# A hybrid encoder layer: background work paced by estimated VectorE time, eight gate tiles moved to seven-product blocks, and an earlier reload of m

## The chip, the cores and the metric

One core of a Trainium2 chip runs the whole kernel. TensorE (PE in the profile, PEld for its weight loads) multiplies, VectorE (DVE) and ScalarE (ACT) do element-wise work, GpSimd (POOL) and SyncE (SP) mostly issue transfers. The metric is the device time of one execution in microseconds; the median of the runs counts, lower is better.

## What is computed

One layer with two mixers, for 512 positions of width 2048, in float32, followed by a final RMSNorm:

```python
h = rmsnorm(x, norm_g)
v, bg, cg, za, u, zb, ga, gb = split(h @ w_in)        # 2048 x (4*2048, 2*1024, 2*2048)
ya = ((bg * causal_conv3(cg * v)) * silu(za)) @ w_out_a
yb = gelu(s5_scan(u))                                  # 64 groups, 16 channels, 64 complex states
yb = yb * sigmoid(yb @ w_glu + b_glu)
yb = (yb * silu(zb)) @ w_out_b
m  = sigmoid(ga) * ya + sigmoid(gb) * yb
out = rmsnorm(x + m @ w_o, final_g)
```

## The kernel before

**Arithmetic.** Every operand of a matmul is split into a rounded part `hi` and a remainder `lo`; a product is hi*hi + hi*lo + lo*hi. Activations lie transposed (channels on partitions, the 512 positions along a row), in `pair` tiles with both parts. A weight slot holds 128 x 1024 numbers: one block of 128 output channels by half of the 2048 inputs.

**Weights.** `WStream` walks a fixed list of weight slots. SP loads a raw slot (`w_raw`), ACT rounds it to `w_hi` (L545), DVE subtracts to get `w_lo` (L562). There are four buffers each of `w_hi` and `w_lo`, and `get` prepares two slots ahead of the one in use.

**A plain tile** of 128 outputs takes two `gemm` calls (one for each half of the inputs), each 8 x 3 matmuls of 128x512 (L700 to L702). `gate` (L824 to L828) computes one such tile of g_a or g_b, applies tanh on ACT (L827) and stores it to DRAM from POOL's queue (L828). g_b comes back as `tmp<-gb`, g_a as `ga_r`.

**A block of seven** (`seven`, `product`) computes two tiles at once by seven products instead of eight (a Strassen-Winograd scheme over two output tiles, two input halves and two halves of the positions). A `product` is 8 matmuls of 128x512 (L931) and 8 of 128x256 (L936). DVE forms four sums and differences of weights for each block (`add7`, L492 to L501); ACT copies partial results out of PSUM (L946, L949, L951, L962), DVE adds them into `half` tiles and into the result. The sums of activations (`th7`, `ty7`) are made once by `combine`.

**The stages in order**: u projection and RMSNorm (0 to 98 us); stage 1, plain tiles: 12 tiles of g_a, 16 of g_b, 8 of z_b; the GLU product; W_out_b, 16 tiles of one gemm, then two more tiles of g_a; the four projections cg, v, za, bg in 32 blocks of seven, each group of four followed by convolution, silu and product; the last two tiles of g_a; W_out_a, four plain tiles and six blocks of seven (`wa`), with `mix` forming m and storing it to DRAM; the output projection with W_o, which needs m back from DRAM as `pair` tiles (`reload_m`, tile `m_r`), and the final norm.

**The background.** Work that is not matmul of the main line is written as generators in a list `bg`. `step(n)` is called after each gemm or product and runs generators up to their next `yield`, strictly in list order. In stage 1 the background is the S5 branch: parameters (`ssm_params`), four blocks of 16 groups (`ssm_blocks`), and `gelu`. For each block `front` fetches u and parameters through POOL's queue and prepares small matrices on DVE (`F`, L48 with names `ssm_f`, `ssm_ft`), `pe1` and `pe2` issue the branch's own matmuls, `post` spreads results on ACT, and `scan` builds a rotation table (`ssm_rr`, `ssm_ri`), turns the states, runs the recurrence (L416) and turns them back. `pe2` writes its output to the tile `uy` through POOL's queue. Before the change `step` counted yields:

```python
    def step(n=1.0):
        owed[0] += n
        while owed[0] >= 1.0:
            owed[0] -= 1.0
            while bg:
                try:
                    next(bg[0])
                    break
                except StopIteration:
                    bg.pop(0)
```

The order of the instructions on each engine is fixed when the kernel is built: it follows the order of the program, except that an instruction for which nothing is missing may be put ahead of an earlier one that is expected to wait. An engine then executes its list in order. Two pools of buffers bind too: `c.r4` with 37 slots (raw weights, pairs, all S5 tiles), and `r4b` with 6 slots, from which `wide` tiles come (results of blocks, `half`, `m_r`, `ga_r`, `tb_r`).

Of the kernel before, what the change touches and what calls it, by code (L numbers as in the profile page):

```python
# [16 lines left out]
P = 128  # L17
# [7 lines left out]
T = 4  # L25
# [3 lines left out]
MAGIC = 12582912.0  # L29
RATE = 2.75  # L30
PRATE = 1.0
WARM = 9
NR4 = 37
NA = 12
NAB = 14
NP7 = 4
HL = L // 2

# [3 lines left out]


def _ew(nc):
    v = nc.vector

    def tt(o, a, b, op):
        return v.tensor_tensor(out=o, in0=a, in1=b, op=op)  # L48
# [189 lines left out]
class Block:  # L238
# [13 lines left out]
    def front(self):  # L252
# [22 lines left out]
        shp = [P, QB, NC]  # L275
        ft = self.new([P, QB, 5, NC], "ft")
        for ri in range(2):
            f = self.new([P, QB, 5, NC], "f")
            for tau in range(5):
                pr = c.pw[:, tau, 0, q0:q0 + QB].unsqueeze(2).to_broadcast(shp)  # L280
                pi = c.pw[:, tau, 1, q0:q0 + QB].unsqueeze(2).to_broadcast(shp)
# [97 lines left out]
    def scan(self):  # L379
# [33 lines left out]
        for q in range(QB):  # L413
            g = c.mag[:, q0 + q:q0 + q + 1].to_broadcast([P, NCH])
            for h in (hr, hi):
                nc.vector.tensor_tensor_scan(out=h[:, q, :], data0=g, data1=h[:, q, :],  # L416
                                             initial=0.0, op0=MUL, op1=ADD)
            if q % 2:
                yield
# [159 lines left out]
def hybrid_kernel(ctx: ExitStack, tc: tile.TileContext, xT, x, cvec, fg, wu, wu7, wabc,  # L579
# [63 lines left out]
    for j in range(NAB, KD):  # L643
        for h in range(2):
            W.add(wga[j, h])
# [37 lines left out]

    def step(n=1.0):
        owed[0] += n
        while owed[0] >= 1.0:
            owed[0] -= 1.0
            while bg:
                try:
                    next(bg[0])  # L690
                    break
                except StopIteration:
                    bg.pop(0)

# [104 lines left out]
    def gelu(m):  # L799
        y = uy[:, m].rearrange("p s k -> p k s")  # L800
        t, u = tmp(), tmp()
        t3, u3 = (v.rearrange("p (k s) -> p k s", s=T) for v in (t, u))
        act.activation(t3, y, AF.Square)
        ts(t, t, 0.044715, MUL, 1.0, ADD)
        tt(t3, t3, y, MUL)
        yield
        act.activation(u, t, AF.Tanh, scale=0.7978845608028654)
        stt(t3, u3, 1.0, y, ADD, MUL)
        g = pair()
        split(g, t)  # L810
        yg.append(g)
        yield
# [92 lines left out]
    for j in range(KD):  # L905
        ps = psum()
        gemm(ps, yb, steps=1.2)
        th = gq[j]
# [3 lines left out]
    for j in range(NA, NAB):  # L912
        gate(ga_d[j // 2][:, j % 2], 2.0)
    while bg:
# [6 lines left out]

    def product(ps, acts, first, last, steps=1.0):

# [15 lines left out]

    def seven(name, acts, steps=1.0):  # L940

# [43 lines left out]
    def out_a(cc, b, j):  # L985
        tt(b, b, cc, MUL)
        nc.gpsimd.dma_start(yag_d[j // 2], b)
        yield

    hb = blocks(hp, th7)  # L990
    for j in range(0, KD, 2):
# [58 lines left out]

    def reload_m(i):
        t = wide("m_r")
        nc.gpsimd.dma_start(t, m_d[i])
# [195 lines left out]
```

## Time and profile before

| | before |
|---|---|
| median of three runs | 1692.85 us (1689.97 to 1694.98) |
| profiled execution | 1694.92 us, its span 1693.1 us |
| mean granted TensorE clock | 0.995 |
| PE, DVE, ACT, POOL busy | 99%, 76%, 43%, 8% of the span |
| HBM read and written | 203.1 and 24.8 MB, 135 GB/s |

The profiled execution is one run. A busy PE is a PE with a matmul in its pipeline; the mean duration of one matmul (390 ns) is longer than the distance between two starts (227 ns), since they overlap. Lines of the page name the source line, the engine, the tile written and the tiles read. An idle time is put down to what ended it last.

### The profile page before, as it was taken

What the parts mean: (1) busy time and instruction counts of PE and PEld (TensorE: products, weight loads), DVE (VectorE), ACT (ScalarE), POOL (GpSimd) and SP (SyncE); (2) the same over time, 40 slices, a digit from 0 to 9 for tenths busy, and PEclk for the clock granted to TensorE, in tenths of its full rate; (3) what the DMA queues carried; (4) which work ended last, traced back from release to release, by engine and by line L of the source; (5) the groups of instructions that cost most, each with busy time, mean ns of one, the idle gap of its engine ahead of it and who ended that gap; (6) DMA issues with size and microseconds to landing.
All of it is one profiled execution on the core that took longest, in us unless ns stands there. A gap on an engine that the chain in (4) does not pass through costs nothing.

```text
span 1693.1 us, 22360 instructions
## 1 busy us (share of the span) xinstructions
PE 1675.1 (99%) x8612; PEld 1434.0 (85%) x8612; DVE 1286.4 (76%) x1889; ACT 722.4 (43%) x941; POOL 138.9 (8%) x240
## 2 busy tenths in 40 slices
PE   9999999999999999999999999999999999999997
PEld 7888888888888888888888888888888888878887
DVE  7895483948769777698989899998989699974333
ACT  6433423334316422454545554445545444453321
POOL 0003203040100021000000000000000220020000
PEclk9999999999999999999999999999999999999999
DMA  8324345353531454233333433333343855576212
GB/s 303 112 89 133 102 147 113 136 145 103 171 112 54 153 172 157 90 118 116 100 112 102 136 128 108 112 99 115 121 132 130 300 196 179 185 266 256 75 38 100
DMA packets 68331, 233.53 MB, mean 138 GB/s; under 512 B 9152, under 2 KB 9280, under 8 KB 68224
## 3 DMA queue, kind: packets, MB, share of 16 engines
q1 hardware_dynamic: 49392, 170.94, 30.2%
q0 software_dynamic: 18112, 60.06, 11.2%
q8 instruction: 67, 1.10, 0.3%
q10 hardware_dynamic: 720, 1.10, 0.2%
q14 instruction: 40, 0.33, 0.1%
HBM read 203.10 MB, written 24.77 MB: 135 GB/s over the span
## 4 chain that ended last, share of the span: by engine, by line
PE 92%; DVE 4%; DMA 2%; issue 1%; ACT 0%; DVEq 0%; POOL 0%; SPq 0%; ACTq 0%; POOLq 0%
PE ps L931 25%; PE ps L936 13%; PE ps L702 12%; PE ps L701 12%; PE ps L700 12%; PE ps L1103 3%; PE ps L1104 3%; PE ps L1102 3%; PE ps L778 1%; PE ps L779 1%; PE ps L777 1%; DVE w_lo L562 1%; DMA w_raw<-in_wga_dram 1%; PE ps L339 1%; PE ps L434 1%
## 5 line engine op out<-in xcount | busy, mean ns | idle before, releaser
L545 ACT CAST w_hi<-w_raw 128x1024 fp32r<-128x1024 f32 (+2 forms) x347 | 361.7, 1043 | 592.9 <-PE ps L701 246.2
L562 DVE TENSOR_TENSOR w_lo<-w_raw,w_hi 128x1024 fp32r<-128x1024 f32 (+2 forms) x347 | 418.5, 1210 | 242.6 <-ACT w_hi L545 241.9
L700 PE MATMUL ps<-pair,w_hi 128*128 128x512 f32 x912 | 355.8, 390 | 0.0
L702 PE MATMUL ps<-pair,w_lo 128*128 128x512 f32 x912 | 354.4, 389 | 0.7 <-DVE w_lo L562 0.7
L701 PE MATMUL ps<-pair,w_hi 128*128 128x512 f32 x912 | 354.7, 389 | 0.0
L931 PE MATMUL ps<-h_comb,w_hi 128*128 128x512 f32 x1216 | 305.3, 393 | 4.7 <-ACT half L951 4.2
L931 PEld LDWEIGHTS ps<-h_comb,w_hi 128*128 128x128 f32 x1216 | 218.9, 189 | 44.5 <-ACT half L951 4.6
L931 PE MATMUL ps<-pair,w_hi 128*128 128x512 f32 x912 | 230.1, 394 | 0.0
L702 PEld LDWEIGHTS ps<-pair,w_lo 128*128 128x128 f32 x912 | 171.2, 188 | 36.4 <-DVE w_lo L562 1.1
L700 PEld LDWEIGHTS ps<-pair,w_hi 128*128 128x128 f32 x912 | 171.3, 188 | 35.1
L701 PEld LDWEIGHTS ps<-pair,w_hi 128*128 128x128 f32 x912 | 171.3, 188 | 35.1
L931 PEld LDWEIGHTS ps<-pair,w_hi 128*128 128x128 f32 x912 | 165.3, 190 | 29.9
L936 PEld LDWEIGHTS ps<-h_comb,w_lo 128*128 128x128 f32 x1216 | 165.9, 190 | 11.9
L936 PE MATMUL ps<-h_comb,w_lo 128*128 128x256 f32 x1216 | 169.6, 282 | 0.0
L545 ACT CAST w_hi<-w_sum 128x1024 fp32r<-128x1024 f32 x76 | 79.9, 1051 | 139.4 <-DVE w_sum L501 61.5
L936 PEld LDWEIGHTS ps<-pair,w_lo 128*128 128x128 f32 x912 | 125.2, 191 | 9.0
L936 PE MATMUL ps<-pair,w_lo 128*128 128x256 f32 x912 | 127.8, 283 | 0.0
L562 DVE TENSOR_TENSOR w_lo<-w_sum,w_hi 128x1024 fp32r<-128x1024 f32 x76 | 92.6, 1218 | 7.2 <-ACT w_hi L545 7.2
L48 DVE TENSOR_TENSOR half<-ps,half 128x512 f32<-128x512 f32 x114 | 78.0, 684 | 7.2 <-PE ps L936 7.2
L1102 PE MATMUL ps<-w_hi,pair 128*128 128x512 f32 (+1 forms) x212 | 81.6, 385 | 0.0
L1103 PE MATMUL ps<-w_lo,pair 128*128 128x512 f32 (+1 forms) x212 | 81.6, 385 | 0.0
L1104 PE MATMUL ps<-w_hi,pair 128*128 128x512 f32 (+1 forms) x212 | 81.6, 385 | 0.0
(197 smaller groups left out, 1784.5 us busy)
## 6 DMA issues: line engine op xcount, KB each, us to landing
w_raw<-in_wabc_dram SPq DMA_DIRECT2D x128, 512.0 KB, 4.2
w_raw<-in_wga_dram SPq DMA_DIRECT2D x64, 512.0 KB, 4.3
w_raw<-in_wgb_dram SPq DMA_DIRECT2D x48, 512.0 KB, 4.2
w_raw<-in_wo_dram SPq DMA_DIRECT2D x32, 512.0 KB, 7.3
w_raw<-in_wgz_dram SPq DMA_DIRECT2D x24, 512.0 KB, 3.6
w_raw<-in_wu_dram SPq DMA_DIRECT2D x15, 448.0 KB, 7.5
xt<-in_xT_dram SPq DMA_DIRECT2D x16, 256.0 KB, 6.5
ga<-tmp POOLq DMA_DIRECT2D x16, 256.0 KB, 2.4
```

Source lines behind the costliest of these rows:

```text
L48: return v.tensor_tensor(out=o, in0=a, in1=b, op=op)
L339: nc.tensor.matmul(ps[:, i * NCH:(i + 1) * NCH], self.sl[ri][:, q].rearrange("p g s -> p (g s)"), self.u4[:, q, :], start=True, stop=True)
L545: nc.scalar.copy(hi[:, a:b], raw[:, a:b])
L562: nc.vector.tensor_tensor(out=lo[:, a:b], in0=raw[:, a:b], in1=hi.bitcast(F32)[:, a:b], op=SUB)
L700: nc.tensor.matmul(ps, hi[:, k], a[:, 0], start=first and k == 0, stop=False)
L701: nc.tensor.matmul(ps, hi[:, k], a[:, 1], start=False, stop=False)
L702: nc.tensor.matmul(ps, lo[:, k], a[:, 0], start=False, stop=last and k == 7)
L931: nc.tensor.matmul(ps if flat else both, hi[:, k], a, start=first and k == 0, stop=False, skip_group_check=True)
L936: nc.tensor.matmul(ps[:, HL:], lo[:, k], a[:, :HL] if flat else a[:, 0], start=False, stop=last and k == 7, skip_group_check=True)
L1102: nc.tensor.matmul(ps, a[:, 0, cs], hi[:, k2, c0:c1], start=first and k2 == 0, stop=False)
L1103: nc.tensor.matmul(ps, a[:, 0, cs], lo[:, k2, c0:c1], start=False, stop=False)
L1104: nc.tensor.matmul(ps, a[:, 1, cs], hi[:, k2, c0:c1], start=False, stop=last and k2 == 1)
```

## The change

1. **Pacing.** The helpers `tt`, `ts`, `stt` and the scan add an estimate of their VectorE time to `SPENT` (0.1 us and 0.00104 us an element of the row). `step(n)` now runs background until the estimated time of what it ran reaches n, counting at least 0.6 us for each yield. All rates are given anew in that unit.
2. **Gate tiles.** Eight tiles of g_a (6 to 13) are no longer plain: four blocks of seven are inserted among the projections, after the second to the fifth group, with `gate2` for tanh and store. Stage 1 keeps four tiles of g_a, tiles 4 and 5 follow W_out_b, 14 and 15 stay.
3. **Reload of m.** `reload_m(a, b)` issues the loads two blocks ahead of the casts. During the last `wa` block it handles tiles 0 and 1; tiles 2 to 6 come after that block, and so does the last `fetch_m`. The other `fetch_m` calls come one block earlier.
4. **Smaller edits.** `F` is computed with 640 elements a row at once instead of five times 128; `gelu` first copies its operand from the strided `uy` to a contiguous tile on ACT.

```diff
-RATE = 2.75
-PRATE = 1.0
+RATE = 4.75
+PRATE = 2.0
-NA = 12
-NAB = 14
+NA = 4
+NAB = 6
+NB7 = 14
+LEAST = 0.6
+R7, RM7 = 1.2, 1.6
+SPENT = [0.0]
+def spend(ap, n=1):
+    size = 1
+    for d in ap.shape[1:]:
+        size *= d
+    SPENT[0] += n * (0.1 + 0.00104 * size)
...
+        p5 = [c.pw[:, :, i, q0:q0 + QB].rearrange("p t q -> p q t").unsqueeze(3).to_broadcast(sh5) ...]
+        c5 = [v.unsqueeze(2).to_broadcast(sh5) for v in (cr, ci)]
         for ri in range(2):
-            f = self.new([P, QB, 5, NC], "f")
-            for tau in range(5):
-                ...
-                tt(ft[:, :, tau, :], ci, pi if ri == 0 else pr, MUL)
-                tt(f[:, :, tau, :], cr, pr if ri == 0 else pi, MUL)
-                if tau == 2:
-                    yield
+            f = self.new(sh5, "f")
+            tt(ft, c5[1], p5[1 - ri], MUL)
+            tt(f, c5[0], p5[ri], MUL)
+            yield
...
     for j in range(0, KD, 2):                       # order of the weights
         for i in range(4):
             W.add7(wabc[j, i, 0], wabc[j + 1, i, 0], wabc[j + 1, i, 1], wabc[j, i, 1])
+        i = NAB + j - 2
+        if NAB <= i < NB7:
+            W.add7(wga[i, 0], wga[i + 1, 0], wga[i + 1, 1], wga[i, 1])
...
     def step(n=1.0):
         owed[0] += n
-        while owed[0] >= 1.0:
-            ...
+        while owed[0] > 0.0 and bg:
+            t = SPENT[0]
+            try:
+                next(bg[0])
+                owed[0] -= max(SPENT[0] - t, LEAST)
+            except StopIteration:
+                bg.pop(0)
+        owed[0] = min(owed[0], n)
...
     def gelu(m):
-        y = uy[:, m].rearrange("p s k -> p k s")
+        y, t, u = tmp(), tmp(), tmp()
+        act.copy(y.rearrange("p (k s) -> p k s", s=T), uy[:, m].rearrange("p s k -> p k s"))
...
-        gemm(ps, yb, steps=1.2)                     # W_out_b
+        gemm(ps, yb, steps=2.4)
-        gate(ga_d[j // 2][:, j % 2], 2.0)           # tiles NA to NAB
+        gate(ga_d[j // 2][:, j % 2], 3.0)
...
+    def gate2(o, j):
+        t = wide("tz")
+        act.activation(t, o, AF.Tanh, scale=0.5)
+        nc.gpsimd.dma_start(ga_d[j // 2], t)
+        yield
...
         b = seven("bg", hb)
         bg.append(out_a(cc, b, j))
+        i = NAB + j - 2
+        if NAB <= i < NB7:
+            bg.append(gate2(seven("ga", hb), i))
...
-        gemm(ps, yap[:8], last=False, steps=3.2)    # and the second half alike
+        gemm(ps, yap[:8], last=False, steps=3.6)
...
-    def reload_m(i):
-        t = wide("m_r")
-        nc.gpsimd.dma_start(t, m_d[i])
-        yield
-        for n in range(2):
-            p = pair()
-            split(p, t[:, n])
-            mp.append(p)
-            yield
+    def reload_m(a, b):
+        q = []
+        for i in range(a, b + 2):
+            if i < b:
+                q.append(wide("m_r"))
+                nc.gpsimd.dma_start(q[-1], m_d[i])
+                yield
+            if i >= a + 2:
+                t = q[i - a - 2]
+                for n in range(2):
+                    ...
...
+    fetch_m()
     for j in range(NP7, KD, 2):
-        fetch_m()
-        if j == KD - 2:
-            for i in range(4):
-                bg.append(reload_m(i))
-        o = seven("wa", yb7, 2.7 if j == KD - 2 else 1.0)
+        end = j == KD - 2
+        if end:
+            bg.append(reload_m(0, 2))
+        o = seven("wa", yb7, RM7 if end else R7)
+        if end:
+            bg.append(reload_m(2, 7))
+            fetch_m()
+            while bg:
+                step()
+        elif j < KD - 4:
+            fetch_m()
         bg.append(mix(o, *mq[j // 2], j))
-    for i in range(4, 7):
-        bg.append(reload_m(i))
```

More of the change, by code (lines that the diff above doesn't have):

```diff
@@ L47, in tt @@
     def tt(o, a, b, op):
+        spend(o)
         return v.tensor_tensor(out=o, in0=a, in1=b, op=op)
     def ts(o, a, s1, op0, s2=None, op1=None):
+        spend(o)
         if op1 is None:
@@ L55, in stt @@
     def stt(o, a, s, b, op0, op1):
+        spend(o)
         return v.scalar_tensor_tensor(out=o, in0=a, scalar=s, in1=b, op0=op0, op1=op1)
@@ L276, in front @@
         ft = self.new([P, QB, 5, NC], "ft")
+        sh5 = [P, QB, 5, NC]
+        p5 = [c.pw[:, :, i, q0:q0 + QB].rearrange("p t q -> p q t").unsqueeze(3).to_broadcast(sh5)
+              for i in range(2)]
+        c5 = [v.unsqueeze(2).to_broadcast(sh5) for v in (cr, ci)]
         for ri in range(2):
-            f = self.new([P, QB, 5, NC], "f")
-            for tau in range(5):
-                pr = c.pw[:, tau, 0, q0:q0 + QB].unsqueeze(2).to_broadcast(shp)
-                pi = c.pw[:, tau, 1, q0:q0 + QB].unsqueeze(2).to_broadcast(shp)
-                tt(ft[:, :, tau, :], ci, pi if ri == 0 else pr, MUL)
-                tt(f[:, :, tau, :], cr, pr if ri == 0 else pi, MUL)
-                if tau == 2:
-                    yield
+            f = self.new(sh5, "f")
+            tt(ft, c5[1], p5[1 - ri], MUL)
+            tt(f, c5[0], p5[ri], MUL)
+            yield
             if ri == 0:
@@ L415, in scan @@
             for h in (hr, hi):
+                spend(h[:, q, :], 2)
                 nc.vector.tensor_tensor_scan(out=h[:, q, :], data0=g, data1=h[:, q, :],
@@ L642, in hybrid_kernel @@
             W.add7(wabc[j, i, 0], wabc[j + 1, i, 0], wabc[j + 1, i, 1], wabc[j, i, 1])
-    for j in range(NAB, KD):
+        i = NAB + j - 2
+        if NAB <= i < NB7:
+            W.add7(wga[i, 0], wga[i + 1, 0], wga[i + 1, 1], wga[i, 1])
+    for j in range(NB7, KD):
         for h in range(2):
@@ L685, in step @@
         owed[0] += n
-        while owed[0] >= 1.0:
[L687 to L693, printed above, removed]
+        while owed[0] > 0.0 and bg:
[6 more added lines that the diff above has]
+        owed[0] = min(owed[0], n)
     def gemm(ps, acts, first=True, last=True, steps=0.0):
@@ L799, in gelu @@
     def gelu(m):
-        y = uy[:, m].rearrange("p s k -> p k s")
-        t, u = tmp(), tmp()
-        t3, u3 = (v.rearrange("p (k s) -> p k s", s=T) for v in (t, u))
-        act.activation(t3, y, AF.Square)
+        y, t, u = tmp(), tmp(), tmp()
+        act.copy(y.rearrange("p (k s) -> p k s", s=T), uy[:, m].rearrange("p s k -> p k s"))
+        act.activation(t, y, AF.Square)
         ts(t, t, 0.044715, MUL, 1.0, ADD)
-        tt(t3, t3, y, MUL)
+        tt(t, t, y, MUL)
         yield
         act.activation(u, t, AF.Tanh, scale=0.7978845608028654)
-        stt(t3, u3, 1.0, y, ADD, MUL)
+        stt(t, u, 1.0, y, ADD, MUL)
         g = pair()
@@ L920, in blocks, with product @@
         return y + [[sums[k][i] for k in range(8)] for i in range(4)]
-    def product(ps, acts, first, last, steps=1.0):
+    def product(ps, acts, first, last, steps=R7):
         hi, lo = W.get()
@@ L938, in product, with seven @@
         step(steps)
-    def seven(name, acts, steps=1.0):
+    def seven(name, acts, steps=R7):
         Y11, Y21, Y22, T1, T2, T3, T4 = acts
@@ L1018, in hybrid_kernel @@
         step()
-    for j in range(NAB, KD):
-        gate(ga_d[j // 2][:, j % 2], 4.0)
+    for j in range(NB7, KD):
+        gate(ga_d[j // 2][:, j % 2], 3.2)
     while bg:
@@ L1040, in hybrid_kernel @@
         ps = psum()
-        gemm(ps, yap[:8], last=False, steps=3.2)
-        gemm(ps, yap[8:], first=False, steps=3.2)
+        gemm(ps, yap[:8], last=False, steps=3.6)
+        gemm(ps, yap[8:], first=False, steps=3.6)
         g, t = (v[:, j % 2] for v in mq[j // 2])
@@ L1049, in hybrid_kernel @@
     mp = []
-    def reload_m(i):
-        t = wide("m_r")
-        nc.gpsimd.dma_start(t, m_d[i])
-        yield
-        for n in range(2):
-            p = pair()
-            split(p, t[:, n])
-            mp.append(p)
-            yield
+    def reload_m(a, b):
[8 more added lines that the diff above has]
+                for n in range(2):
+                    p = pair()
+                    split(p, t[:, n])
+                    mp.append(p)
+                    yield
     def mix(o, g, t, j):
```

## The prediction

> **What bounds the kernel now.** I read the totals first, then the chain that ended last, the waits of PE, and the busy time by stage.
>
> ```profile
> span 1693.1 us, 22360 instructions
> ...
> PE 1675.1 (99%) x8612; PEld 1434.0 (85%) x8612; DVE 1286.4 (76%) x1889; ACT 722.4 (43%) x941; POOL 138.9 (8%) x240
> ...
> PE 92%; DVE 4%; DMA 2%; issue 1%; ACT 0%; DVEq 0%; POOL 0%; SPq 0%; ACTq 0%; POOLq 0%
> ```
> ```profile
> PE ps L931 <- ACT half L951: 4.2, 1, 4.2
> PE ps L777 <- ACT pair L760: 2.5, 1, 2.5
> ...
> PE ps L702 <- DVE w_lo L562: 0.7, 1, 0.7
> PE ps L931 <- DVE half L48: 0.6, 1, 0.6
> ```
> ```profile
> 98.00:541.00 443.00, 442.31 (x2178) 374.51 (x2177) 306.62 (x692) 164.36 (x228) 79.22 (x125) 1.00 0.40 120
> ...
> 590.00:672.00 82.00, 82.00 (x363) 67.91 (x362) 58.41 (x93) 24.16 (x30) 16.73 (x31) 1.00 0.51 169
> ...
> 694.00:1319.00 625.00, 625.00 (x3583) 550.05 (x3582) 558.79 (x570) 314.42 (x377) 5.34 (x10) 1.00 0.36 118
> ```
> PE is the bound nearly everywhere: it waits about 9 us in all, half of that in one place (ACT's copy at L951, near 1492 us). So the time falls only by matmuls taken away or by that one wait, and rises only where another engine makes PE wait anew. In the third fence each row is a stage: width, then busy PE, PEld, DVE, ACT, POOL. Stage 1 (98 to 541: gates, zb, the S5 background) has DVE 69% busy, the four-projection stage (694 to 1319) 89%.
>
> **The change, part by part.** Price of PE work first. ACT's gate tanh (L827) follows each pair of plain weight tiles; the products of a seven-product block follow each other in the chain.
>
> ```profile
> 282.33 0.60 ACT L827 ACTIVATE tmp<-ps 128x512 f32<-128x512 f32 x1 [4.61 <-PE ps L702]
> 293.21 0.60 ACT L827 ACTIVATE tmp<-ps 128x512 f32<-128x512 f32 x1 [9.35 <-PE ps L702]
> ```
> ```profile
> 696.32 1.84 PE ps L931 x8
> 699.12 1.84 PE ps L931 x8
> ```
> One gate tile is 293.21 - 282.33 = 10.88 us of PE (48 matmuls); one product is 2.793 us (the stage has 32 x 7 = 224 of them: 625/224 = 2.79). Eight plain gate tiles cost 8 x 10.88 = 87.0 us, four blocks of seven products 4 x 7 x 2.793 = 78.2 us. **PE loses 8.8 us.** No matmul is added elsewhere.
>
> The price on the other engines, from the groups of instructions:
>
> ```profile
> L562 DVE TENSOR_TENSOR w_lo<-w_raw,w_hi 128x1024 fp32r<-128x1024 f32 x330 | 401.0, 1219 | 232.4 <-ACT w_hi L545 231.8
> L492 DVE TENSOR_TENSOR w_sum<-w_raw 128x1024 f32<-128x1024 f32 x38 | 46.5, 1225 | 13.2 <-DMA w_raw<-in_wabc_dram 7.8 <-DMA w_raw<-in_wga_dram 4.7
> L48 DVE TENSOR_TENSOR half<-ps,half 128x512 f32<-128x512 f32 x114 | 78.0, 684 | 7.2 <-PE ps L936 7.2
> L48 DVE TENSOR_TENSOR cg<-half 128x512 f32<-128x512 f32 x16 | 11.0, 688 | 0.0
> L48 DVE TENSOR_TENSOR ssm_ft<-ssm_bc,ssm_keep 128x128 f32<-128x128 f32 x56 | 14.2, 281 | 8.3 <-DMA ssm_bc<-in_ce_dram 8.3
> L48 DVE TENSOR_TENSOR ssm_f<-ssm_f,ssm_ft 128x640 f32<-128x640 f32 x4 | 3.3, 813 | 0.0
> L48 DVE TENSOR_TENSOR tmp<-tmp,uy 128x512 f32<-128x512 f32 x8 | 8.8, 1099 | 0.2
> L803 ACT ACTIVATE tmp<-uy 128x512 f32<-128x512 f32 x8 | 9.2, 1153 | 3.9 <-DMA uy<-ssm_y 3.9
> ```
> A block of seven needs 7 w_lo, 4 sums, 3 adds on half and 2 adds into the result: 7 x 1.22 + 4 x 1.22 + 3 x 0.68 + 2 x 0.69 = 16.8 us of DVE in 19.55 us of PE. Four more bring the projection stage to 558.8 + 67 = 626 of 703 us, 89% as before; 32 such blocks run there with PE busy all 625 us, so I cost it at nothing. Without that cover the price is the excess of DVE over PE, which at 89% is none. The gate's tanh there (ACT) and its store (POOL) replace two each in stage 1.
>
> Stage 1 shrinks by 87 us to 356 us and must still hide all the background. DVE there loses 16 w_lo (19.5 us), in F 80 x 0.281 becomes 16 x 0.813 (-9.5 us), and two gelu operands become contiguous (1.10 to 0.68 us each, 16 of them, -6.6 us): 306.6 - 35.6 = 271 us of 356, 76%. ACT gets 8 copies of about 1.15 us (as L803, which reads the same strided operand): +9 us, with ACT busy 164 of 443 now. By the change's own estimate (0.1 + 0.00104 per element, at least 0.6 a step) the background is 39.9 (parameters) + 4 x 50.7 (blocks) + 2.4 + 20.2 (gelu) = 265 us. Supplied are 6 x 2.0 in the u projection and 56 x 4.75 = 266 in stage 1: it runs out some 2 gemms (5.44 us each, half a gate tile) before the end. Before it was 198 steps against 6 + 72 x 2.75 = 204, also 2 gemms. So none is left over for the bare loop behind the stage.
>
> What can make PE wait is the order. Between blocks, u must go out and come back through POOL's queue before DVE can begin F of the next block; w_lo queue behind F and what follows.
>
> ```profile
> 265.71 0.48 PE L700 MATMUL ps<-pair,w_hi 128*128 128x512 f32 x1
> 299.35 0.39 PE L702 MATMUL ps<-pair,w_lo 128*128 128x512 f32 x1
> ```
> ```profile
> 277.75 1.23 DVE L562 TENSOR_TENSOR w_lo<-w_raw,w_hi 128x1024 fp32r<-128x1024 f32 x1 [4.21 <-ACT w_hi L545]
> 285.93 0.29 DVE L48 TENSOR_TENSOR ssm_ft<-ssm_bc,ssm_keep 128x128 f32<-128x128 f32 x1 [6.96 <-DMA ssm_bc<-in_ce_dram]
> ...
> 297.56 1.22 DVE L562 TENSOR_TENSOR w_lo<-w_raw,w_hi 128x1024 fp32r<-128x1024 f32 x1
> ...
> 300.48 0.07 DVE L387 MEMSET ssm_rr<- 128x8 f32 x1
> ...
> 317.37 2.35 DVE L48 TENSOR_TENSOR ssm_t<-ssm_h,ssm_ri 128x1024 f32<-128x1024 f32 x2
> ...
> 336.04 3.49 DVE L562 TENSOR_TENSOR w_lo<-w_raw,w_hi 128x1024 fp32r<-128x1024 f32 x3
> ```
> The second block's state output ends at 265.7; F starts 20.2 us later; the next w_lo ends at 298.78 and PE uses it at 299.35: only 0.6 us to spare. In the new pacing an empty step costs 0.6 of 4.75, so F is issued 7.9/4.75 = 1.7 gemms after the scan's end instead of 12/2.75 = 4.4, and the next scan's rotation table (ssm_rr) follows it sooner. The 20 us are POOL's chain and stay; F is 1 us shorter; the table (about 8 us) may now come ahead of a w_lo that PE needs. Bounds per handover: a gain of 0 (nothing waits there now) and a loss of 8 us; two handovers have the next block's F in them and are this tight. The nearest rows are the ones above, where the w_lo (297.56) came ahead of the table (300.5), so I take 1 us each, **+2 us**, and keep 0 to 16. The pace of 2.0 in the u projection adds some 3 us to a DVE that has slack; the wait of 0.7 on w_lo behind it stays: 0, at most 1. In the W_out_b stage the eight sums are 8 x 4.0 = 32 us by the same estimate, supply 16 x 2.4 = 38, DVE 71% busy now: 0. The other changed paces move order alone: 0, and up to 1 either way.
>
> m reloaded. Around the one long wait of PE:
>
> ```profile
> 1488.52 2.00 PE L931 MATMUL ps<-h_comb,w_hi 128*128 128x512 f32 x8
> ...
> 1496.60 1.22 PE L931 MATMUL ps<-h_comb,w_hi 128*128 128x512 f32 x2 [4.19 <-ACT half L951]
> 1497.62 3.62 PE L931 MATMUL ps<-pair,w_hi 128*128 128x512 f32 x8
> 1501.03 1.74 PE L936 MATMUL ps<-pair,w_lo 128*128 128x256 f32 x8
> ```
> ```profile
> 1485.61 0.53 POOL L1053 DMA_DIRECT2D m_r<-m  x1 [1.00 <-DVE wa L48]
> ```
> ```profile
> 1493.98 1.14 ACT L616 CAST pair<-m_r 128x512 fp32r<-128x512 f32 x2 [4.79 <-DMA m_r<-m]
> ...
> 1495.97 0.57 ACT L951 COPY half<-ps 128x512 f32<-128x512 f32 x1
> 1496.45 0.58 ACT L949 COPY half<-ps 128x512 f32<-128x512 f32 x1
> ```
> ```profile
> m_r<-m POOLq DMA_DIRECT2D x7, 512.0 KB, 7.6
> ```
> ACT stands in order at the cast of m_r, whose load takes 8.3 us, and the copies that free PSUM (L949, L951) stand behind it. PE loses 4.19, and then 1.6 + 0.6 + 0.6 because the same eight matmuls take 3.62 instead of 2.00 us after the gap: 7.0 us. The change issues two loads first and casts in the third product's step, behind L949 but still ahead of L951, and leaves the last gate and tb loads (two of the six r4b buffers) until after the block. The third product ends near 1491.3 and its copy is needed near 1494.1; a load issued at 1485.6 lands at 1493.9, so 0.5 to 2.4 us of waiting are left. The other loads then come behind the block, each needed 5.4 us after the last, which 7.6 us loads two in flight can hold. Bounds: 0 (the wait only moves to L951; a loss would need later loads) and 7.0; I take **-5.0 us**.
>
> The Trainium skill (DMA: Bandwidth & Descriptors, the SWDGE path) fits such a transfer as about 2.0 us plus bytes over 436 GB/s, an estimate of 3.2 us for 512 KB; by it the whole 7.0 us would return and the sum below be 2 us lower. The rows say 7.6, and the sum goes by them.
>
> Sum: -8.8 + 2.0 - 5.0 = -11.8 us. The profiled execution took 1694.92 us (its span 1693.1 and 1.8 around it) and would take 1683.1; the median of the three runs is 2.1 us lower, 1692.85, and gives **1681 us**.
>
> **The rivals.**
> (a) All goes well: no handover waits, the 7.0 us and the 0.7 return: -16.5, 1676 us. For it: in the list of PE's waits stage 1 has only the 0.7. Against: ACT's casts still precede L951.
> (b) The m wait stays or moves: -8.8 + 2 = -6.8, 1686 us. For it: 7.6 us loads against 5.7 us between issue and need.
> (c) The handovers eat the gain: 4 to 5 us at two of them, -8.8 - 5 + 9, 1688 us. For it: the 0.6 us to spare. Against: the table stood behind the w_lo in the rows. The Trainium skill (TensorE: Matmul & The Clock Gate, Part 1) halves PE's clock after an idle window of about 3.4 us; by it a handover under that costs only itself. The 3.62 against 2.00 us agree.
> (d) Slower: DVE bounds stage 1. A gemm's ration is 4.75 x 1.05 (1.22 us measured for 1024 elements, 1.165 estimated) + 1.22 = 6.2 us against 5.44 of PE; the scan part is 32 us of estimate in each of four blocks, 27 gemms x 0.76 = 20 us, 1692.85 - 13.8 + 20 = 1699 us. It decides once w_lo has no lead left; against it, the rows from 317.37 to 336.04 hold 18.7 us of DVE without one w_lo and PE did not wait.
>
> **How the numbers follow.** Likeliest 0.37, (a) 0.17, (b) 0.21, (c) 0.16, (d) 0.09. A measurement of this kernel can tell about 0.3% (5.1 us) from no change, so below 1687.8 is faster: 0.37 + 0.17 + 0.21 = 0.75; (c) is the same, 0.16; (d) slower, 0.09. The range runs from (a) less the 2.9 us by which the fastest run lies under the median, 1673, to (c) with both handovers at their 8 us bound and some of the m wait, about 1694; it leaves out (d) and the ends.
>
> **What would show it.** Right: PE busy lower by about 9 us; 42 blocks of seven; no wait of PE at L949 or L951 over 2.5 us; F in stage 1 still some 20 us behind the state output. Wrong: waits of PE on w_lo between 200 and 420 us summing over 5 us, DVE over 95% in stage 1, or a new wait of PE on m pairs at the start of the output projection.

## The result and the profile after

The changed kernel takes 1698.94 us (median of 11 runs, 1694.54 to 1708.1), the kernel before 1693.55 (11 runs beside them): a ratio of 1.0041, 95% interval 1.0026 to 1.0057. It is 0.4% slower, where 1681 us was forecast. The profiled execution took 1699.68 us, its span is 4.7 us longer than that of before. One run of experiment 7, of 8757.76 us, stands apart from its eleven others and is left out of the time given there.

The page, its totals and the two groups of the products in blocks of seven (L952, formerly L931):

```profile
span 1697.8 us, 22501 instructions
...
PE 1671.1 (98%) x8676; PEld 1431.3 (84%) x8676; DVE 1320.2 (78%) x1873; ACT 745.5 (44%) x973; POOL 136.6 (8%) x236
...
L952 PE MATMUL ps<-h_comb,w_hi 128*128 128x512 f32 x1344 | 337.0, 392 | 3.5 <-ACT half L972 2.2
...
L952 PE MATMUL ps<-pair,w_hi 128*128 128x512 f32 x1008 | 252.3, 392 | 0.0
```

1344 + 1008 = 2352 matmuls of that line are 42 blocks of 7 x 8, as the change says. PE is busy for 4.0 us less, not 9 (matmuls at a slow pace, shown below, count as busy), and idle for 8.7 us more (26.7 against 18.0). The list of PE's waits says where (who waited for whom, the sum in us, how often, the longest; w_hi is now L563, w_lo L580, the copies of partial results L967 and L972, gelu's pairs L634 and L63):

```profile
PE ps L724 <- DVE w_lo L580: 4.5, 3, 2.4
...
PE ps L952 <- ACT half L972: 2.2, 1, 2.2
PE ps L356 <- ACT ssm_sl L343: 2.0, 1, 2.0
PE ps L722 <- ACT w_hi L563: 1.6, 1, 1.6
PE ps L722 <- ACT pair L634: 1.1, 2, 0.8
...
PE ps L723 <- DVE pair L63: 1.0, 2, 0.8
PE ps L952 <- ACT half L967: 0.9, 1, 0.9
PE ps L452 <- DVE ssm_h L63: 0.5, 1, 0.5
```

The wait at the reload of m is down from 4.2 to 2.2 us. Grown in stage 1 is w_lo (0.7 before); new there are ssm_sl, w_hi and ssm_h, and behind it, at the start of the GLU product, the pairs of gelu. Busy time by stage (width, then PE, PEld, DVE, ACT, POOL), stage 1 up to the GLU product, the GLU stage, and the projections:

```profile
98.00:469.00 371.00, 362.35 (x1811) 306.07 (x1810) 268.95 (x574) 143.81 (x207) 74.83 (x117) 1.00 0.39 116
469.00:516.00 47.00, 44.91 (x187) 35.90 (x187) 35.17 (x48) 22.63 (x32) 0.00 (x0) 0.96 0.30 97
...
622.00:1325.00 703.00, 702.76 (x4024) 618.20 (x4023) 620.23 (x632) 355.45 (x424) 7.48 (x14) 1.00 0.36 119
```

The projections hide four more blocks with 0.24 us of idle PE in 703 us. In stage 1 and at the GLU start PE is idle for 10.7 us, with VectorE 72% busy in stage 1 (268.95 of 371): it is not the bound.

By the distances between starts of matmuls (0.226 us for 128x512 where nothing waits) the two executions differ so:

| | us |
|---|---|
| eight tiles by seven products | -8.8 |
| reload of m (7.0 lost before, 2.4 after) | -4.6 |
| stage 1 (0.6 lost before, 11.7 after: 2.4 at 156 us, 1.6 at 259, 1.1 at 295, 6.1 at 333 to 341, small ones 0.5) | +11.1 |
| start of the GLU product, 470 to 478 us | +4.8 |
| first 100 us (+0.7), projections and W_out_a (+1.3) | +2.0 |
| sum, and the measured difference of the spans | +4.5, +4.7 |

The largest place, first on PE, then on ACT (tanh of a gate tile is L848), on VectorE, and in the DMA queue of SP:

```profile
332.84 0.39 PE L724 MATMUL ps<-pair,w_lo 128*128 128x512 f32 x1
334.85 0.50 PE L722 MATMUL ps<-pair,w_hi 128*128 128x512 f32 x1 [1.62 <-ACT w_hi L563]
335.19 0.40 PE L723 MATMUL ps<-pair,w_hi 128*128 128x512 f32 x1
337.94 0.80 PE L724 MATMUL ps<-pair,w_lo 128*128 128x512 f32 x1 [2.36 <-DVE w_lo L580]
338.54 0.63 PE L722 MATMUL ps<-pair,w_hi 128*128 128x512 f32 x1
338.96 0.63 PE L723 MATMUL ps<-pair,w_hi 128*128 128x512 f32 x1
...
341.41 0.39 PE L723 MATMUL ps<-pair,w_hi 128*128 128x512 f32 x1
341.63 0.39 PE L724 MATMUL ps<-pair,w_lo 128*128 128x512 f32 x1
```
```profile
311.28 1.05 ACT L563 CAST w_hi<-w_raw 128x1024 fp32r<-128x1024 f32 x1 [4.38 <-PE ps L723]
312.36 0.60 ACT L848 ACTIVATE tmp<-ps 128x512 f32<-128x512 f32 x1
322.39 0.60 ACT L848 ACTIVATE tmp<-ps 128x512 f32<-128x512 f32 x1 [9.43 <-PE ps L724]
333.27 0.60 ACT L848 ACTIVATE tmp<-ps 128x512 f32<-128x512 f32 x1 [10.28 <-PE ps L724]
333.76 1.04 ACT L563 CAST w_hi<-w_raw 128x1024 fp32r<-128x1024 f32 x1
...
342.67 1.05 ACT L563 CAST w_hi<-w_raw 128x1024 fp32r<-128x1024 f32 x1 [1.00 <-DMA w_raw<-in_wgb_dram]
```
```profile
336.06 0.69 DVE L63 TENSOR_TENSOR ssm_t<-ssm_wb,ssm_bs 128x512 f32<-128x512 f32 x1 [8.79 <-ACT ssm_sl L343]
336.67 1.22 DVE L580 TENSOR_TENSOR w_lo<-w_raw,w_hi 128x1024 fp32r<-128x1024 f32 x1
```
```profile
301.71 0.33 SPq L545 DMA_DIRECT2D w_raw<-in_wgb_dram  x1
...
326.89 0.33 SPq L545 DMA_DIRECT2D w_raw<-in_wgb_dram  x1
```

Between 312.33 and 333.76 us ACT makes no w_hi: three tanh stand in a row, and the second and third each wait some 10 us for the end of their own tile on PE, ahead of the next cast. PE works off the weights that were ready, ends the tile at 333, and only then tanh, w_hi and w_lo follow, while PE waits 1.62 and 2.36 us and runs for 3 us at half pace (starts 0.427 apart). VectorE was idle for 8.79 us before that: the first w_lo stands there behind a product that waits for ssm_sl, from ACT as well.

The weights of that cast had long landed. Each cast takes the next load in turn: the cast at 342.67, which waits for its load, takes the one issued at 339.40, so the three casts before it (333.76, 335.93, 340.64) take those of 301.71, 302.25 and 326.89. The load of 301.71 landed 3.2 us later, 29 us before its cast, and the late load of 326.89 is not the one that PE waits for here. At 156 us it is the same engine in a shorter form: ssm_sl (L343) stands behind a tanh that waits for PE, and PE stands at the matmuls that read it.

```profile
156.31 0.60 ACT L848 ACTIVATE tmp<-ps 128x512 f32<-128x512 f32 x1 [3.96 <-PE ps L724]
156.94 1.33 ACT L343 ACTIVATE ssm_sl<-ssm_t,cvec_t 128x512 f32<-128x512 f32 x2
```

At the GLU start gelu is late. Its first and its last instruction on ACT and VectorE:

```profile
439.44 1.11 ACT L823 COPY tmp<-uy 128x512 f32<-128x512 f32 x1 [5.13 <-DMA uy<-ssm_y]
```
```profile
473.20 0.69 DVE L63 TENSOR_TENSOR pair<-tmp,pair 128x512 fp32r<-128x512 f32 x1 [0.19 <-ACT pair L634]
```

The same two in the kernel before:

```profile
507.88 1.13 ACT L803 ACTIVATE tmp<-uy 128x512 f32<-128x512 f32 x1 [3.86 <-DMA uy<-ssm_y]
```
```profile
541.56 0.69 DVE L48 TENSOR_TENSOR pair<-tmp,pair 128x512 fp32r<-128x512 f32 x1
```

From the landing of the last state output to the last pair it takes 34.5 us now and took 34.4 before (507.88 to 542.25). The length is the same, the matmuls left beside it are not: the GLU product began 33 us after gelu in the kernel before, and begins 26 us after it now.

### The profile page after: what moved, and what is told of

It reads as the page before. It is cut to its first block, busy times and chain, and to the rows that moved or that the text cites. A ratio compares the mean times of both kernels' runs of the same rounds, so it can differ in the third digit from the quotient of the medians.

```text
span 1697.8 us, 22501 instructions
## 1 busy us (share of the span) xinstructions
PE 1671.1 (98%) x8676; PEld 1431.3 (84%) x8676; DVE 1320.2 (78%) x1873; ACT 745.5 (44%) x973; POOL 136.6 (8%) x236
## 5 line engine op out<-in xcount | busy, mean ns | idle before, releaser
L563 ACT CAST w_hi<-w_raw 128x1024 fp32r<-128x1024 f32 (+2 forms) x351 | 364.9, 1042 | 497.4 <-PE ps L723 120.6
L580 DVE TENSOR_TENSOR w_lo<-w_raw,w_hi 128x1024 fp32r<-128x1024 f32 (+2 forms) x351 | 422.8, 1210 | 203.2 <-ACT w_hi L563 200.0
L952 PE MATMUL ps<-h_comb,w_hi 128*128 128x512 f32 x1344 | 337.0, 392 | 3.5 <-ACT half L972 2.2
L724 PE MATMUL ps<-pair,w_lo 128*128 128x512 f32 x784 | 306.8, 392 | 4.5 <-DVE w_lo L580 4.5
L722 PE MATMUL ps<-pair,w_hi 128*128 128x512 f32 x784 | 307.2, 392 | 2.7 <-ACT w_hi L563 1.6
L723 PE MATMUL ps<-pair,w_hi 128*128 128x512 f32 x784 | 306.2, 391 | 1.0 <-DVE pair L63 1.0
L952 PEld LDWEIGHTS ps<-h_comb,w_hi 128*128 128x128 f32 x1344 | 241.6, 189 | 47.6 <-ACT half L972 2.4
L952 PE MATMUL ps<-pair,w_hi 128*128 128x512 f32 x1008 | 252.3, 392 | 0.0
L952 PEld LDWEIGHTS ps<-pair,w_hi 128*128 128x128 f32 x1008 | 181.4, 189 | 32.5
L957 PEld LDWEIGHTS ps<-h_comb,w_lo 128*128 128x128 f32 x1344 | 183.4, 190 | 13.1
L957 PE MATMUL ps<-h_comb,w_lo 128*128 128x256 f32 x1344 | 187.4, 282 | 0.0
L724 PEld LDWEIGHTS ps<-pair,w_lo 128*128 128x128 f32 x784 | 147.9, 189 | 36.6 <-DVE w_lo L580 6.2
L722 PEld LDWEIGHTS ps<-pair,w_hi 128*128 128x128 f32 x784 | 148.0, 189 | 34.0 <-ACT w_hi L563 2.0
L723 PEld LDWEIGHTS ps<-pair,w_hi 128*128 128x128 f32 x784 | 148.0, 189 | 32.4 <-DVE pair L63 1.6
L563 ACT CAST w_hi<-w_sum 128x1024 fp32r<-128x1024 f32 x84 | 88.4, 1052 | 158.2 <-DVE w_sum L519 72.9
L957 PEld LDWEIGHTS ps<-pair,w_lo 128*128 128x128 f32 x1008 | 137.5, 190 | 9.8
L957 PE MATMUL ps<-pair,w_lo 128*128 128x256 f32 x1008 | 140.5, 282 | 0.0
L580 DVE TENSOR_TENSOR w_lo<-w_sum,w_hi 128x1024 fp32r<-128x1024 f32 x84 | 102.3, 1217 | 4.2 <-ACT w_hi L563 4.2
L63 DVE TENSOR_TENSOR half<-ps,half 128x512 f32<-128x512 f32 x126 | 86.2, 684 | 5.9 <-PE ps L957 5.9
```

The costliest lines, as they stand in the source:

```text
L563: nc.scalar.copy(hi[:, a:b], raw[:, a:b])
L580: nc.vector.tensor_tensor(out=lo[:, a:b], in0=raw[:, a:b], in1=hi.bitcast(F32)[:, a:b], op=SUB)
L722: nc.tensor.matmul(ps, hi[:, k], a[:, 0], start=first and k == 0, stop=False)
L723: nc.tensor.matmul(ps, hi[:, k], a[:, 1], start=False, stop=False)
L724: nc.tensor.matmul(ps, lo[:, k], a[:, 0], start=False, stop=last and k == 7)
L952: nc.tensor.matmul(ps if flat else both, hi[:, k], a, start=first and k == 0, stop=False, skip_group_check=True)
```

## The experiments

Two theories stood at first. P: the new pacing makes the losses, since steps without VectorE work count little. S: the shorter stage makes them, whatever the pacing. "Counted steps" is the pacing of before. Ratios are to the kernel before, run beside each.

**1. The small parts alone** (steps12): counted steps at 2.75, NA, NAB = 12, 14; new reload, F and gelu kept.

> The kernel before with the small parts of the change alone: m reloaded early, F in five-wide operations, gelu with its copy. Pacing still counts steps (2.75 a gemm), all 12 gate tiles stay in stage 1. The trace of the changed kernel shows 2.3 us of wait left at the reload of m where 7.0 were lost, and 18 us of new losses of PE elsewhere (12 at four places of stage 1, 5 at the start of the GLU stage, 1 to 2 later). Theory P (the pacing by estimated time makes the losses: a step without VectorE work counts only 0.6 of 4.75, so the parts of the S5 branch that hang on each other are issued too close) and rival S (the shorter stage 1 makes them, whatever the pacing: the same background in 56 gemms instead of 72) both give 1693.5 - 4.7 = 1689 us here. 1694 or more would mean that one of the small parts itself costs time.

1689.81 us, 0.9977 (0.9966 to 0.9988). No small part costs; in its trace PE waits only 0.7 us in stage 1.

**2. The move with counted steps** (steps4):

```diff
-        while owed[0] > 0.0 and bg: ...        # estimated time
+        while owed[0] >= 1.0: ...              # counted steps, RATE = 3.6
```

> The changed kernel with the pacing of before: steps are counted, 3.6 a gemm, so that the background of 192 steps ends about 2.5 gemms before the end of the 56 gemms, as before. Eight gate tiles in blocks of seven, the other parts as changed. P: the losses go, 1689 - 8.8 = 1680 us. S: the 12 us of stage 1 and the 5 of the GLU start stay, 1695 to 1699 us.

1704.64 us, 1.0067 (1.0055 to 1.0079): 5.7 us slower than the changed kernel, and beyond what S expected too. P falls: the trace loses 10.9 us in stage 1 and 6.8 at the GLU start, about as with pacing by time (11.7 and 4.8). Another 6.1 us are lost at the reload of m (2.4 in the changed kernel), whose paces were changed too, so the run does not say which pacing is better.

**3. Pacing by time without the move** (time12): `NA, NAB, RATE = 12, 14, 3.65`.

> The changed kernel with all 12 gate tiles back in stage 1 and no gate tile in the added blocks of seven: pacing by estimated time at 3.65 a gemm, which supplies the 253 us of stage 1 some 2.5 gemms before its end. P: the handovers still lose, 6 to 12 us, so 1695 to 1701 us. S: nothing waits, 1689 us as with counted steps.

1689.71 us, 0.9985 (0.9972 to 0.9997), the same as counted steps. Pacing by time costs nothing and gains nothing here.

**4. Half of the move** (time8): `NA, NAB, RATE = 8, 10, 4.1`.

> The changed kernel with half of the move: 8 gate tiles of g_a in stage 1, four in two blocks of seven, estimated time at 4.1 a gemm (64 gemms). PE work is 4.4 us less than before, the reload gains 4.7. P: 1684.5 + 12 to 17 = 1697 to 1701 us. S: about half of the 17 us or less, 1685 to 1693 us.

1698.96 us, 1.0035 (1.0021 to 1.0049). The time is in P's range, but 2 and 3 speak against P; S's range is missed. It is as slow as the whole move: 4.9 us are lost in stage 1, 7.8 at the GLU start and 6.2 at the reload of m (its profiled execution, 1702.25 us, is 3.3 above the median). The losses are not in proportion to the move.

What sorts these four is the amount of background issued per gemm: nothing is lost at 3.65 (2.75 counted steps are about as much), much from 4.1 on. Theory R: it is that density. Its test leaves PE's work and the length of the stage alone.

**5. Only the rate** (time12_fast), `RATE = 3.65` to `4.75` in the kernel of 3:

> The kernel with pacing by time, all 12 gate tiles in stage 1 and none in the added blocks (1689.7 us at 3.65 a gemm), now at the rate of the changed kernel, 4.75 a gemm: the background ends some 19 gemms before the end. Theory R (it is the amount of background issued per gemm that makes the losses of stage 1: steps that hang on each other by transfers and by ACT stand fewer microseconds apart): the 8 to 12 us at the handovers come back, none at the GLU start, 1698 to 1702 us. Rival M (the moved tiles do it in another way, by the order of weights and buffers or by the shorter stage as such): no losses, 1689.7 us.

1710.55 us, 1.0101 (1.0087 to 1.0115): 20.8 us more than at 3.65, and more than expected; the trace loses 17 us more in stage 1, and 5.4 at the reload of m, where time12 lost nothing. The waits of PE in stage 1, at 4.75 and (second fence) the busy time of the stage at 3.65:

```profile
PE ps L724 <- DVE w_lo L580: 8.0, 5, 3.8
PE ps L722 <- ACT w_hi L563: 2.2, 2, 1.6
PE ps L356 <- ACT ssm_sl L343: 2.0, 1, 2.0
```
```profile
98.00:541.00 443.00, 442.23 (x2178) 374.36 (x2177) 289.45 (x592) 166.87 (x234) 79.62 (x125) 1.00 0.40 120
```

With twelve plain tiles in stage 1 and no tile moved, the places of the changed kernel come back (155, 258, 335 us; two more at 468 and 480). The density alone brings the losses of stage 1, without a moved tile. That the moved tiles act by nothing else is not shown by it.

**6. The same move, but four more gemms in stage 1** (na6): `NA, NAB = 6, 6`.

> The changed kernel with gate tiles 4 and 5 in stage 1 instead of behind W_out_b, nothing else: the same work of PE, the same rate of 4.75, but the GLU product begins 4 gemms (21.8 us) later beside the same background. In the four traces so far the gelu part takes 32 to 36 us from the landing of the last state output to the last pair, whatever the pacing. R: the 4.8 us at the GLU start go, the 12 at the handovers stay, 1694 us. M: also the handovers change, or nothing does.

1698.59 us, 1.0032 (1.0020 to 1.0044). The waits at the GLU start are gone as expected, but the time is not: PE now loses 2.1 us at the first projections, behind W_out_b, where the two tiles had stood, and 4.1 instead of 1.6 at 258 us.

**7. The same with another order in the S5 branch** (na6_table):

```diff
     yield from blocks[0].front()
+    for _ in range(2):
+        SPENT[0] += RATE
+        yield
...
-            yield from blocks[i + 1].front()
-        yield from k.scan()
+            front = blocks[i + 1].front()
+            yield next(front)              # the loads
+            for _ in range(7):
+                yield next(scan)           # the rotation table
+            yield from front
+        yield from scan
```

> The same with two changes of order in the S5 branch: the rotation table of a block's scan (7 steps of VectorE work that needs no transfer) is issued between the loads of the next block and its F, and two gemms without background stand ahead of the first block's matmuls. R: F and the first block's matmuls no longer stand where their inputs are late; of the 12 us at the handovers (2.4 at 156 us, 6.1 at 333, the rest small) 8 or more go, 1684 to 1687 us. If the weights wait for buffers that the next block holds, whatever the order, the loss at the second handover stays: 1691 us.

1690.83 us (1691.29 as the median of all twelve), 0.9984 (0.9973 to 0.9995), 7.8 us less than 6. The wait at 156 is gone, that of the second handover is 1.4 instead of 6.7 us; 2.9 at 267 and the wait behind W_out_b stay, and the profiled execution lost 5.0 at the reload of m. The time is above the 1687 of R and beside the 1691 of its rival, but by number alone: the loss that the rival said would stay is nearly gone.

**8 to 10. Is it buffers?** held12, fast36 and fast38 take away or add one of the shared buffers:

```diff
+    held = c.r4.tile([P, SLOT], F32, tag="r4", name="held")     # held12, fast36: until the GLU stage
...
-        bs = self.new([P, QB, 2, NP], "bs")                      # fast38
+        bs = self.c.sx.tile([P, QB, 2, NP], F32, tag="sx", name="ssm_bs")
```

> The kernel with pacing by time at 3.65 and all 12 gate tiles in stage 1 (1689.7 us), with one of the 37 buffers that weights and S5 tiles share taken away for the length of stage 1. In the changed kernel no load of weights is issued between 302.3 and 326.9 us, for want of a buffer. Theory B (buffers are the limit at the handovers): PE waits there now, 4 us or more, 1694 us or above. If the order of instructions on ACT and VectorE is the limit: at most 1 us, 1690 us.

1691.27 us, 0.9988 (0.9976 to 1.0001): no wait in stage 1 but the 0.8 us of every kernel.

> The kernel with 12 gate tiles in stage 1 and the rate of the changed kernel (4.75 a gemm, 1710.6 us; PE loses 16.8 us at five places between 154 and 482 us), with one of the 37 shared buffers taken away in stage 1. Theory B (at this rate the weights' loads stand behind the buffers of the next block, and what PE waits for are late loads): the losses at 258 and 335 us grow by 5 us or more together, 1716 us or above. If it is the order of instructions on ACT and VectorE alone: within 2 us of 1710.6.

1707.43 us, 1.0081 (1.0062 to 1.0099): no loss grows with a buffer less, against B (2.0 instead of 5.4 us at 258, 6.1 as before at 335). It is 3.1 us below time12_fast, where the other forecast allowed 2.

> The same kernel with one buffer more: ssm_bs, one of the tiles of the branch, gets a place of its own, and the pool tmp has three buffers for it instead of five (which can slow gelu, here far from the GLU product, and the norm in the first 98 us). Theory B: the losses at 258 and 335 us (11.6 us) shrink by 5 us or more, 1705 us or below. If the order alone is the limit: 1710 us, the same places in the trace.

1714.04 us, 1.0111 (1.0095 to 1.0128), 4 us above the forecast for order alone, with 5.0 us of one new wait at 478 us, beside gelu, which has fewer tmp buffers there. At 331 us PE loses 6.8 us (6.1 in time12_fast). Loads of weights and ACT there, in fast38 (tanh is L850):

```profile
300.26 0.33 SPq L545 DMA_DIRECT2D w_raw<-in_wgb_dram  x1
...
312.39 0.33 SPq L545 DMA_DIRECT2D w_raw<-in_wgb_dram  x1
```
```profile
311.13 0.60 ACT L850 ACTIVATE tmp<-ps 128x512 f32<-128x512 f32 x1
321.16 0.60 ACT L850 ACTIVATE tmp<-ps 128x512 f32<-128x512 f32 x1 [9.43 <-PE ps L726]
332.09 0.60 ACT L850 ACTIVATE tmp<-ps 128x512 f32<-128x512 f32 x1 [10.33 <-PE ps L726]
332.58 1.04 ACT L563 CAST w_hi<-w_raw 128x1024 fp32r<-128x1024 f32 x1
```

With one buffer more the late load goes out at 312.39 instead of 330.54 in time12_fast, and the loss stays. Counted as above, the cast at 332.58 takes the load of 300.26, landed at 303.46; it runs 29 us later, behind the third tanh. So buffers do not make PE wait at this place, and the late load was no more than a companion. Whether they had a part in the order that was chosen when the kernel was built is not shown. Theory O: the order of ACT's list, fixed when the kernel is built.

**11 and 12. Other orders.** lead3 changes one number of the changed kernel, `WStream(c, 2, 2)` to `WStream(c, 2, 3)`.

> The changed kernel with one number altered: a weight slot is loaded three operations ahead instead of two. Theory O (what PE waits for at the handovers is the order of ACT's list, fixed when the kernel is built: tanh of a gate tile, which waits for PE, stands ahead of the casts w_hi of weights that have landed). In ACT's list of the changed kernel two tanh in a row have no cast between them and the next one none again at the place of the 6.1 us wait; with the earlier loads no two such gaps follow each other. O: the 6.1 us at 333 us go, 1693 us. If buffers were the limit, one slot more in use would cost: 1699 us or above.

1696.98 us, 1.0019 (1.0010 to 1.0028). Waits in stage 1 of lead3, and below those of order6:

```profile
PE ps L452 <- DVE ssm_h L63: 3.2, 4, 2.1
PE ps L356 <- ACT ssm_sl L343: 2.0, 1, 2.0
PE ps L722 <- ACT pair L634: 1.3, 1, 1.3
...
```
```profile
PE ps L730 <- ACT pair L642: 1.7, 2, 0.9
PE ps L731 <- DVE pair L63: 0.8, 1, 0.8
PE ps L732 <- DVE w_lo L588: 0.7, 1, 0.7
```

In lead3 the waits on w_hi and on w_lo at 259 and 333 us are gone, as O says, but 4.9 us are lost at 300 to 310 us on ssm_h (1.1 in the changed kernel): the branch's own matmuls now stand ahead of the scan that they read. That takes back half of the 7.7 us recovered, and the time stays above the 1693 expected. order6 takes 6 tiles in stage 1, the order of 7, three slots ahead, the mended reload (below), at 4.4 a gemm.

> The kernel with 6 gate tiles in stage 1, three blocks of seven (PE work 6.6 us less), scan table ahead of F and mended reload (1690.6 us; its ACT list has two gaps of casts in a row, and PE lost 5.8 us in stage 1), now with weights loaded three operations ahead, one idle gemm instead of two, and 4.4 a gemm. In ACT's list every two tanh have at least one cast between them up to the last tile. O: no wait of PE above 1 us in stage 1; 1688.0 (the best so far, with 12 tiles there) - 6.6 = 1681 us, up to 1684 if the GLU start waits. If the rate alone counts (4.1 lost 5 us in stage 1 and 7.8 at the GLU start): 1688 or more.

1689.65 us, 0.9974 (0.9965 to 0.9984). No wait in stage 1 up to the GLU product, as O says; its forecast of the time failed, since gelu is late again (the pairs' waits, 6.0 us lost with the slow pace) and the profiled execution (1694.08, the slowest of nine) also lost 9.9 us in the first 21 (7.0 in the kernel before) and 4.6 at 1395. Rate and order were both changed in it, so it doesn't tell them apart.

The traces of all runs point the same way at the largest places. Three tanh in a row with no cast between them stand, ahead of 400 us, in seven kernels (changed, time12_fast, na6, fast36, fast38, and time10_m and best6 below). Each time 3.6 to 6.9 us are lost behind them, with the weights of the next cast landed 25 to 30 us before it. Two in a row cost nothing in time12, held12 and time12_m; elsewhere losses stand near some of them (5.4 us at 262 in time12_fast).

**13. The reload of m** (time12_m) in the kernel of 3:

```diff
             if i >= a + 2:
+                if i == 3:
+                    for _ in range(14):
+                        yield
```

> The kernel with pacing by time at 3.65 and all 12 gate tiles in stage 1 (1689.7 us median, single runs 1686.6 to 1695.8), with the casts of the second tile of m moved behind ACT's copy of the fourth product in the last block, nothing else. In the traces so far PE lost 0 to 5.4 us behind those casts, 7 with the slow clock after it, since the second load waits for a buffer and lands late. Theory W (that wait comes and goes from run to run and explains the runs at 1694 to 1696): the upper runs go, 1687 us, all within 1686 to 1690. Rival: the spread comes from elsewhere, 1689.7 with the same spread.

1687.96 us, all six runs within 1687.24 to 1688.65, 0.9971 (0.9960 to 0.9982). The narrower spread is what theory W says, and the five runs of 14 show it too (1687.04 to 1690.09); no run at 1694 to 1696 was profiled. ACT and POOL in the kernel of 4 (time8), then ACT in this one:

```profile
1504.22 1.14 ACT L634 CAST pair<-m_r 128x512 fp32r<-128x512 f32 x2 [6.75 <-DMA m_r<-m]
1506.21 0.57 ACT L972 COPY half<-ps 128x512 f32<-128x512 f32 x1
```
```profile
1494.59 0.53 POOL L1086 DMA_DIRECT2D m_r<-m  x1 [8.48 <-DVE wa L63]
```
```profile
1491.95 0.59 ACT L972 COPY half<-ps 128x512 f32<-128x512 f32 x1
1495.61 1.14 ACT L634 CAST pair<-m_r 128x512 fp32r<-128x512 f32 x2 [0.72 <-DMA m_r<-m]
```

The second load of m was meant to go out with the first; POOL holds it for 8.5 us until a `wide` buffer is free. It then took 9.6 us (1494.59 to 1504.2) in time8 and 5.5 in steps12, where PE did not wait. With the casts behind the copy its length no longer matters.

**14. The mended reload alone, in the kernel before** (before_m):

> The kernel before with the early reload of m alone, in the mended form (casts of the second tile behind the copy of the fourth product): counted steps, F and gelu as before, no gate tile moved. If the reload is all that the small parts gain, 1688 us as with all of them (1688.0); if F and gelu gain too, 1689 or more.

1688.59 us, 0.9968 (0.9955 to 0.9980): the whole gain of the small parts is the reload; F and gelu give nothing that can be told.

**15 to 18. Is a part of the move to be had?** time10_m is the kernel of 13 with `NA, NAB, RATE = 10, 12, 3.85`. best12, best6 and best5 have the order of 7 and the mended reload, with NA, NAB, RATE of 12, 14, 3.8; 6, 8, 4.7; 5, 6, 4.9.

> The kernel of 1688.0 us (pacing by time, mended reload, 12 gate tiles in stage 1) with 10 tiles in stage 1 at 3.85 a gemm and two tiles in one block of seven: PE work 2.2 us less. Theory R: 3.85 is near 3.65, where nothing waits, and far from 4.1, where 13 us are lost: 1686 to 1688 us. If any move of a tile costs: 1690 us or more.

1695.04 us, 1.0004 (0.9995 to 1.0013): one block of seven, 2.2 us of work less, and 7.1 us slower than 13; 6.0 us are lost at 283 to 291 us behind three tanh without a cast between them, and 5.0 at 1396 (its profiled execution, 1698.31 us, is the slowest of eleven). R, taken as a smooth rule, fails here.

> The same with the table of the scan issued ahead of the next block's F and two idle gemms ahead of the first block's matmuls, at 3.8 a gemm: no gate tile moved. Nothing waited there at this rate, so 1687 us, as without the new order. If the rate is the cause and the order only its cure, there is no gain here; if the order had cost time before the change too, 1684 us or less.

1690.45 us, 0.9985 (0.9976 to 0.9993): above the 1687 expected, with two waits of 1.2 us on w_hi at 293 and 383 us. The new order is no gain here; as the rate differs too (3.8 for 3.65), what made these waits is not told apart.

> New order in the S5 branch and the later casts of m, with 6 gate tiles in stage 1 at 4.7 a gemm, 2 behind W_out_b, 6 in three blocks of seven, 2 plain ones at the end. PE work 6.6 us below before. From 1691.3 (same order, tiles 4 and 5 in stage 1, four blocks of seven): 2.2 more PE work, 2.3 less at the end of W_out_b, 2 to 3 less at m: 1688 to 1689 us by theory R; 1684 if the rate just below 4.75 frees the two handovers that still lost 4.4.

1690.62 us, 0.9989 (0.9978 to 1.0000), above the 1688 to 1689 expected: 3.9 us of waits on w_hi stay.

> The same with 5 gate tiles in stage 1 at 4.9 a gemm, 1 behind W_out_b, all eight in four blocks of seven. PE work 8.8 us below before. From 1691.3: 2.3 less at the end of W_out_b, 2 to 3 less at m, 0 to 4 more at the handovers by the higher rate: 1687 to 1691 us by R.

1697.19 us, 1.0024 (1.0012 to 1.0035), above the range expected: 3.9 at 335, 3.0 more with the slow pace behind it, 8.2 at 468 to 485 us.

The fastest versions by their medians are 13 and 14, level within their intervals: all gate tiles where they were, and the reload of m in its mended form, 5 us below the kernel before. order6, with six tiles moved and the same reload, lies within these intervals too (0.9974): there the 6.6 us of work saved are about what gelu loses at the GLU start (6.0).

## Why the prediction was wrong

- **PE loses 8.8 us: right.** 42 blocks of seven, and the projections hide them (0.24 us idle in 703).
- **m, -5.0: right in size, wrong in one step.** The change gained 4.6 in the profiled execution; the small parts alone 4.0, the mended reload 5. But of the "two loads first" the second went out 8.5 us later, held by a buffer.
- **Stage 1, +2.0: the step that failed.** It took one handover's rows of the old pacing (a margin of 0.6 us) and gave 1 us to each of two. It measured +11.1, inside the bounds 0 to 16 that were worked out and then left. The mechanism differed too. The prediction looked on VectorE, for a rotation table ahead of a w_lo; at 333 us PE waited first for w_hi, behind three tanh in ACT's list, while VectorE was idle for 8.79 us. At 156 us it was ssm_sl behind a tanh, for which the sum had no term. The figures for the density were on the table: the same 253 us of estimate, ended some 2.5 gemms early, are 4.75 a gemm in 56 gemms and some 3.65 in 72, and experiment 5 shows that this ratio alone costs more than 11 us. The mean load of VectorE (76% forecast, 72% measured) could not show it. As far as the traces at 156 and 333 us go, what lacks is not time on an engine but distance between steps that hang on each other through ACT and PE.
- **"None is left over for the bare loop": true of the issue, not of the work; the second step that failed, a term put at nothing.** The last steps were issued some 2 gemms ahead, but gelu needs 34 us from its first input, and only 26 were left: +4.8 (with four gemms more ahead of the GLU product, experiment 6, it is gone). The copies in gelu, costed at nothing, were rightly so (34.5 against 34.4 us).
- **The rivals.** (c) named the handovers at 9 us, about what those of 259 to 341 us measured (8.8), though not for its reason; the time went past it by the first block, the GLU start and the smaller places. (d) gave 1699 us, the time measured, by luck: its mechanism, VectorE as the bound, did not hold (72%). The upper end of the range, 1694, was also set too low by its own terms: -8.8 - 5.0 + 16 is 1695 us, before any of the m wait is added. The Trainium skill's clock gate (TensorE: Matmul & The Clock Gate, Part 1), as used under (c), did not hold: waits of 1.6 and 2.4 us, each under its window of about 3.4 us, cost 6.1 together.
- **The tests.** F began 17.5 us behind the state output (301.68 to 319.21), near the 20 named. The test "w_lo waits over 5 us between 200 and 420" would not have pointed it out (3.7), since the loss is spread over w_lo, w_hi, ssm_sl, ssm_h and the slow pace. The sign "PE busy lower by about 9 us" did fail (4.0).

What is shown: density alone can make the loss of stage 1 (3 against 5), a buffer less or more does not change it at 333 us (8 to 10), and there the cast that PE waits for stands behind a tanh that waits for PE, with its weights landed 29 us before; with another order the wait goes (lead3). What stays open: why the order comes out so at some densities and not at others (time10_m lost at 3.85 what time12 did not at 3.65), and how much of the loss at the other places has this cause.

## What to carry to other kernels

When main work is taken out of a stage that hides a chain, count the chain's fixed latencies (transfer round trips, the last conversion) in microseconds against what is left beside them, at its start, at each handover and at its end; the mean load of the engines did not show it here (VectorE 72%). Where engines run lists in order, look in the trace for an instruction that waits for the bottleneck engine and has that engine's next operand behind it: three such tanh in a row let PE use up its four prepared weight slots here and cost 6 us. And measure the parts of a change apart: the small one held all of the gain.

## What the runs showed of the hardware

In the changed kernel PE's slow pace did not need one long idle stretch. After waits of 1.62 and 2.36 us with two matmuls between, the starts were 0.427 us apart for about 3 us, with a granted clock of 0.50 from 338 to 341 us. At the GLU start four waits of 0.28, 0.78, 0.81 and 0.23 us within 4.2 us were followed by the same pace and the same clock of 0.50 from 474.6 to 477.6 us. A single wait of 2.04 us (158 us) or 2.15 (1505 us) was not: the clock behind it was 1.00. And the same 512 KB load by POOL's queue took 5.5 us in one kernel and 9.6 in another.
